# Low halves of the split weights: a subtraction on VectorE or GpSimd replaced by a negated copy on ScalarE and an adding DMA

## The chip, the core and the metric

The kernel runs on one core of one Trainium2 chip. The metric is the device time of one execution in microseconds (us). The median of three timed runs of the kernel before the change is 998.04 us (995.92 to 1000.73). The profile below is of another single execution.

## What is computed

One inference step of a hybrid decoder layer for a prompt of 512 tokens and a sample group of 8 x 8 tokens (576 token columns in all) with the same weights:

```python
hn = rmsnorm(x, norm1_w) * (1 + sc1) + sh1
u = hn @ w_in                                    # split into z, xbc, dt, q, k, v, o, ig, fg, xr, gr
y_ssd = ssd_chunked(causal_conv(xbc), dt, ...)   # Mamba-2 heads, states carried over chunks of 128
y_ml = mlstm_chunked(q, k, v, ig, log_sigmoid(fg), ...)
y_lru = lru_scan(causal_conv(xr), ...) * gelu(gr)
x = x + g1 * (concat(y_ssd, y_ml, y_lru) @ w_out)
hn = rmsnorm(x, norm2_w) * (1 + sc2) + sh2
x = x + g2 * (relu(hn @ mlp_up) ** 2 @ mlp_down)
y = rmsnorm(x, final_norm_w)                     # outputs: y and the new states of the three mixers
```

All inputs are float32. The large products keep float32 accuracy by splitting both operands into a high part, rounded to the reduced format fp32r that TensorE multiplies, and a low part, the exact rest. A product is then three matmuls: high x high, high x low, low x high.

## The kernel before

**Blocks and units.** The weights lie in DRAM as 124 blocks of 128 x 1024 numbers (512 KB): eight 128 x 128 tiles, one for each eighth of the contraction. Block 0 is the gates' weights and isn't split. Blocks 1 to 44 belong to `w_in`, 45 to 60 to `w_out`, 61 to 124 to the MLP. One block is one *unit* on TensorE (PE): for each of the eight tiles six matmuls of 288 columns (`mm_k`, L156 to L166, all at L164): two halves of the tokens with the high weights and the high activations, two with the high weights and the low activations, and two with the low weights (`wl`) and the high activations. So the first matmul that reads `wl` is the fifth of its unit, and the unit's last matmul reads it too.

**How a block is made ready.** `w_load` (L122) queues a DMA of the block from SyncE's queue (SP) into a buffer `raw`, of which there are three. `w_prep` (L132) then makes the two parts: ScalarE (ACT) copies `raw` into `wh` with rounding to fp32r (L150), and a subtraction gives `wl = raw - wh` (L152). The subtraction runs on GpSimd (POOL) for blocks 7 to 32 (`WL_POOL`, L1483) and on VectorE (DVE) for the others; block 3 has its own code (L141 to L146). `wh` and `wl` have three buffers each (`W_BUFS`). When PE starts the unit of block b, the program asks for block b + 2 to be prepared (`PREP = 2`), so `wh` and `wl` of b + 2 take the buffers that block b - 1 has just left.

**Stages.** Up to about 60 us: loads, the first norm and modulation, blocks 1 to 3. To about 470 us: the units of `w_in`, with the mixers between them (convolutions, SSD, mLSTM, RG-LRU), called the mixer stage here. Then 16 units of `w_out`, and from about 568 us the MLP. The last units and the final norm end the program.

**What sets the order.** Each engine runs its own queue strictly in order. The queues' order comes from a scheduler with a timing model that runs when the program is built, apart from the first and the last stretch, where the source fixes it. An instruction that waits holds up everything behind it on its engine. For POOL this covers the DMAs that it issues: the scratch stores `scr_cum` (L524), `scr_nm` (L561) and `scr_ends` (L588) and the outputs at L658, L987, L1146 and L1172. In the mixer stage DVE does most of the elementwise work, the convolution at L626 and L651 above all (taps multiplied and added, 128 x 600), and ACT evacuates the convolution's PSUM banks (L611 to L614).

Of the kernel before, what the change touches and what calls it, by code (L numbers as in the profile page):

```python
# [22 lines left out]
FT = mybir.dt.float32  # L23
FR = mybir.dt.float32r
BF = mybir.dt.bfloat16
AF = mybir.ActivationFunctionType
OP = mybir.AluOpType
# [40 lines left out]
class Kernel:  # L68
# [63 lines left out]
    def w_prep(self, upto):  # L132
        nc = self.nc
        while self.w_next_split <= min(upto, NBLK - 1):
            b = self.w_next_split
            self.w_load(b)
            raw = self.w_raw.pop(b)
            m = raw.shape[2]
            if b == 0:
                self.w_split[b] = raw  # L140
            elif b == 3:  # L141
                hl = [[self.T("wt", FR)[:, :512].rearrange("p (k m) -> p k m", k=4) for _ in range(2)] for _ in range(2)]
                for (hi, lo), src in zip(hl, (raw[:, :4], raw[:, 4:])):
                    nc.scalar.activation(hi, src, AF.Copy)
                    nc.vector.tensor_tensor(lo, src, hi.bitcast(FT), op=OP.subtract)
                self.w_split[b] = (lambda k, t=hl: t[k // 4][0][:, k % 4], lambda k, t=hl: t[k // 4][1][:, k % 4], m)  # L146
            else:
                hi = self.wpool.tile([128, 8, m], FR, name=self.name("wh"), tag="wh", bufs=W_BUFS)
                lo = self.wpool.tile([128, 8, m], FR, name=self.name("wl"), tag="wl", bufs=W_BUFS)
                nc.scalar.activation(hi, raw, AF.Copy)  # L150
                eng = nc.gpsimd if b in WL_POOL else nc.vector
                eng.tensor_tensor(lo, raw, hi.bitcast(FT), op=OP.subtract)  # L152
                self.w_split[b] = (lambda k, t=hi: t[:, k], lambda k, t=lo: t[:, k], m)
            self.w_next_split += 1

# [1324 lines left out]
W_BUFS = 3  # L1480
RAW_BUFS = 3
CONV = "addd"
WL_POOL = range(7, 33)  # L1483
ON_POOL = ('fin', 's0', 'S', 'rmax', 'gu1', 'gu2', 'cf2', 'vm')
TAIL = 2, 1, 2

# [152 lines left out]
```

## Time and profile before

| | |
|---|---|
| median of three runs | 998.04 us |
| profiled execution, device time | 995.4 us |
| its span, first to last instruction | 993.6 us |
| PE busy | 959.5 us, 97% |
| DVE / ACT / POOL busy | 590.2 / 399.8 / 203.8 us |
| moved by DMA | 119.62 MB |

The profiled execution took 995.4 us, of which 1.8 us lie outside the span. The median of the timed runs is 2.6 us above it. A row of a group view gives line, engine, operation, written tile <- read tiles, shape, count, busy time and mean duration, and behind the bar the idle time of the engine just before these instructions with what ended it. PE's matmuls overlap in the pipeline, so two that are shown at 0.43 us start 0.27 us apart.

### The profile page before, as it was taken

What the parts mean: (1) busy time and instruction counts of PE and PEld (TensorE: products, weight loads), DVE (VectorE), ACT (ScalarE), POOL (GpSimd) and SP (SyncE); (2) the same over time, 40 slices, a digit from 0 to 9 for tenths busy, and PEclk for the clock granted to TensorE, in tenths of its full rate; (3) what the DMA queues carried; (4) which work ended last, traced back from release to release, by engine and by line L of the source; (5) the groups of instructions that cost most, each with busy time, mean ns of one, the idle gap of its engine ahead of it and who ended that gap; (6) DMA issues with size and microseconds to landing.
All of it is one profiled execution on the core that took longest, in us unless ns stands there. A gap on an engine that the chain in (4) does not pass through costs nothing.

```text
span 993.6 us, 18146 instructions
## 1 busy us (share of the span) xinstructions
PE 959.5 (97%) x7369; PEld 904.1 (91%) x7370; DVE 590.2 (59%) x1180; ACT 399.8 (40%) x741; POOL 203.8 (21%) x220
## 2 busy tenths in 40 slices
PE   8999789889999999999999999999999999999996
PEld 5889778777788899999999999999999999999996
DVE  4669897887788377468444455533553355335544
ACT  3454744453646674345222234312441144114320
POOL 2836454532355532020000000000000000000032
PEclk8999999998999999999999999999999999999998
DMA  9721254654464333444222322222222222222202
GB/s 343 294 86 64 81 186 133 246 173 137 131 223 153 105 137 129 140 131 162 91 98 105 110 86 84 74 79 84 85 86 85 86 85 76 76 83 85 85 23 96
DMA packets 51220, 119.62 MB, mean 120 GB/s; under 512 B 6956, under 2 KB 17468, under 8 KB 51136
## 3 DMA queue, kind: packets, MB, share of 16 engines
q1 hardware_dynamic: 47024, 111.06, 32.7%
q10 hardware_dynamic: 3744, 6.85, 1.8%
q8 instruction: 58, 0.95, 0.4%
q0 software_dynamic: 368, 0.55, 0.2%
q14 instruction: 26, 0.21, 0.1%
HBM read 108.68 MB, written 9.76 MB: 119 GB/s over the span
## 4 chain that ended last, share of the span: by engine, by line
PE 76%; DVE 10%; ACT 4%; issue 3%; DMA 1%; POOL 0%; POOLq 0%; DVEq 0%; ACTq 0%
PE g L164 66%; DVE r L626 3%; PE adap L218 1%; PE g L1363 1%; DMA nmb<-scr_nm 1%; PE py L729 1%; PE lg L1129 1%; DVE att L707 1%; PE ps L734 1%; PE py L732 1%; DVE nmb L924 1%; DVE xbc L651 0%; DVE sp_e L494 0%; PE adas L228 0%; ACT r L620 0%
## 5 line engine op out<-in xcount | busy, mean ns | idle before, releaser
L150 ACT ACTIVATE wh<-raw 128x1024 fp32r<-128x1024 f32 x123 | 130.1, 1058 | 333.9 <-PE g L164 309.4
L164 PE MATMUL g<-hnh,wh 128*128 128x288 f32 x688 | 153.1, 302 | 10.1 <-ACT r L614 8.0
L164 PE MATMUL g<-hnh,wl 128*128 128x288 f32 x688 | 152.1, 299 | 0.6 <-DVE wl L152 0.6
L164 PE MATMUL g<-hnl,wh 128*128 128x288 f32 x688 | 151.8, 299 | 0.0
L152 DVE TENSOR_TENSOR wl<-raw,wh 128x1024 fp32r<-128x1024 f32 x97 | 118.7, 1225 | 29.5 <-ACT wh L150 29.4
L164 PEld LDWEIGHTS g<-hnh,wh 128*128 128x128 f32 x688 | 110.4, 189 | 19.3 <-ACT r L614 9.2
L164 PEld LDWEIGHTS g<-hnh,wl 128*128 128x128 f32 x688 | 111.6, 189 | 2.7 <-issue 1.2
L164 PEld LDWEIGHTS g<-hnl,wh 128*128 128x128 f32 x688 | 111.7, 189 | 0.8 <-issue 0.4
L164 PE MATMUL g<-h2h,wh 128*128 128x288 f32 (+1 forms) x512 | 110.9, 297 | 0.0
L164 PE MATMUL g<-h2l,wh 128*128 128x288 f32 (+1 forms) x512 | 110.9, 298 | 0.0
L164 PE MATMUL g<-h2h,wl 128*128 128x288 f32 (+1 forms) x512 | 110.0, 296 | 0.0
L307 DVE SCALAR_TENSOR_TENSOR xr<-g,modt,xr 128x288 f32<-128x288 f32 x38 | 19.7, 518 | 141.2 <-PE g L164 141.2
L164 PE MATMUL g<-hh,wl 128*128 128x288 f32 x480 | 102.9, 295 | 0.0
L164 PE MATMUL g<-hh,wh 128*128 128x288 f32 x480 | 102.5, 295 | 0.0
L164 PE MATMUL g<-hl,wh 128*128 128x288 f32 x480 | 102.4, 295 | 0.0
L1405 POOL TENSOR_SCALAR xr<-xr,vec 128x576 f32<-128x576 f32 (+2 forms) x8 | 15.2, 1900 | 383.8 <-ACT sqa L1237 363.4
L152 POOL TENSOR_TENSOR wl<-raw,wh 128x1024 fp32r<-128x1024 f32 x26 | 69.0, 2653 | 80.3 <-ACT wh L150 61.4
L164 PEld LDWEIGHTS g<-h2h,wl 128*128 128x128 f32 x512 | 83.4, 188 | 0.0
L164 PEld LDWEIGHTS g<-h2h,wh 128*128 128x128 f32 x512 | 83.1, 189 | 0.1
L164 PEld LDWEIGHTS g<-h2l,wh 128*128 128x128 f32 x512 | 83.0, 188 | 0.0
L164 PEld LDWEIGHTS g<-hh,wh 128*128 128x128 f32 x480 | 77.0, 188 | 0.0
L164 PEld LDWEIGHTS g<-hh,wl 128*128 128x128 f32 x480 | 77.0, 188 | 0.0
(399 smaller groups left out, 1652.7 us busy)
## 6 DMA issues: line engine op xcount, KB each, us to landing
raw<-w SPq DMA_DIRECT2D x124, 512.0 KB, 3.5
ada<-ada SPq DMA_DIRECT2D x32, 512.0 KB, 5.6
ada<-ada SPq DMA_DIRECT2D x32, 256.0 KB, 5.9
cumb<-scr_cum SPq DMA_DIRECT2D x16, 256.0 KB, 5.6
s<-s SPq DMA_DIRECT2D x16, 256.0 KB, 4.7
ssm_s<-s ACTq DMA_DIRECT2D x16, 256.0 KB, 2.9
x<-x SPq DMA_DIRECT2D x8, 288.0 KB, 4.7
xr<-x SPq DMA_DIRECT2D x8, 288.0 KB, 3.9
```

Source lines behind the costliest of these rows:

```text
L150: nc.scalar.activation(hi, raw, AF.Copy)
L152: eng.tensor_tensor(lo, raw, hi.bitcast(FT), op=OP.subtract)
L164: self.nc.tensor.matmul(pg.h[h][:m, :e], w(k), xx[:, h * HALF:h * HALF + e], start=start and n == 0, stop=stop and n == 2)
L218: nc.tensor.matmul(ps[32 * j:32 * j + 32, :256], self.cs[:, k, :], ks(k), start=k < 4, stop=k >= 4)
L307: self.nc.vector.scalar_tensor_tensor(dst[:, :HALF], pg.h[0][:, :HALF], gate[:, 0:1], x[:, :HALF], op0=OP.mult, op1=OP.add)
L626: nc.vector.scalar_tensor_tensor(a[:, :n], r[:, j:j + n], wcols[:, j:j + 1], a[:, :n], op0=OP.mult, op1=OP.add)
L707: self.eng("att").tensor_scalar(E[:, h * 128:(h + 1) * 128], cums[h2][:, h * 128:(h + 1) * 128], self.col1[:, c, hd:hd + 1], 0.0, op0=OP.a ...
L729: nc.tensor.matmul(o, xdt[:, h * 64:(h + 1) * 64], att[h // 4][:, hs], start=True, stop=not c)
L732: nc.tensor.matmul(o, S[:, h * 64:(h + 1) * 64], ce[h // 4][:, hs], start=False, stop=True)
L734: nc.tensor.matmul(pst, cb[:, 128:256], xend[:, :512], start=True, stop=True)
L924: self.eng("nmb").tensor_scalar(E[:, tk(c)], nmb[:, tk(c)], ecol(c), 0.0, op0=OP.add, op1=OP.min)
L1405: self.eng("fin").tensor_scalar(x, x, self.v("fnw")[:, o:o + 1], None, op0=OP.mult)
```

## The change

For blocks 9 to 124 (except that block 3 is untouched anyway) `wl` isn't subtracted any more. ACT makes a second copy of `raw`, with scale -1 and the same rounding, into `wl`, which then holds the negated high part. POOL then issues a DMA that reads the same block from DRAM a second time and adds it to `wl`, element by element (`accum_op`). The sum is again block minus high part. Blocks 1, 2 and 4 to 8 are subtracted on DVE, so blocks 7 and 8 go from POOL to DVE.

```diff
                 nc.scalar.activation(hi, raw, AF.Copy)
-                eng = nc.gpsimd if b in WL_POOL else nc.vector
-                eng.tensor_tensor(lo, raw, hi.bitcast(FT), op=OP.subtract)
+                if b < WL_DMA:
+                    nc.vector.tensor_tensor(lo, raw, hi.bitcast(FT), op=OP.subtract)
+                else:
+                    nc.scalar.activation(lo, raw, AF.Copy, scale=-1.0)
+                    nc.gpsimd.dma_start(lo, self.io["w"][b - 1].rearrange("p (k m) -> p k m", k=8), accum_op=OP.add)
...
-WL_POOL = range(7, 33)
+
+WL_DMA = 9
```

In the changed kernel L154 is the negated copy and L155 the adding DMA; lines behind them are three higher than before, and from L1484 on four.

POOL's queue early in the mixer stage, around the store `scr_nm`, before:

```order
L152 TENSOR_TENSOR wl_1330<-raw_1130,wh_1329 128x1024
L561 DMA scr_nm<-nm_1110 4x576
L565 DMA m_out<-mo 4x9
L609 MEMSET r_1291 128x3
L610 COPY r_1291<-vec 128x8x3
L635 COPY cso<-r_1291 128x27
L588 DMA scr_ends<-ends 36x12
```

and with the change:

```order
L155 DMA wl_1333<-w 128x1024
L564 DMA scr_nm<-nm_1111 4x576
L612 MEMSET r_1294 128x3
L568 DMA m_out<-mo 4x9
L613 COPY r_1294<-vec 128x8x3
L638 COPY cso<-r_1294 128x27
L591 DMA scr_ends<-ends 36x12
```

The issue of the adding DMA stands where the subtraction stood; the two rows of `m_out` and a memset change places.

DVE's queue at the start of the mixer stage, where blocks 7 and 8 are now subtracted, before:

```order
L651 SCALAR_TENSOR_TENSOR xbc_720<-r_707,r_713 128x512
L653 SCALAR_TENSOR_TENSOR xbc_720<-r_707,r_713 128x64
L651 SCALAR_TENSOR_TENSOR xbc_736<-r_723,r_729 128x512
L653 SCALAR_TENSOR_TENSOR xbc_736<-r_723,r_729 128x64
L626 SCALAR_TENSOR_TENSOR r_745<-r_739,cwh,r_745 128x600 x2
L626 SCALAR_TENSOR_TENSOR r_833<-r_827,cwh,r_833 128x600
L626 SCALAR_TENSOR_TENSOR r_745<-r_739,cwh,r_745 128x600
L626 SCALAR_TENSOR_TENSOR r_833<-r_827,cwh,r_833 128x600 x2
```

and with the change:

```order
L654 SCALAR_TENSOR_TENSOR xbc_720<-r_707,r_713 128x512
L656 SCALAR_TENSOR_TENSOR xbc_720<-r_707,r_713 128x64
L152 TENSOR_TENSOR wl_850<-raw_760,wh_849 128x1024
L654 SCALAR_TENSOR_TENSOR xbc_736<-r_723,r_729 128x512
L656 SCALAR_TENSOR_TENSOR xbc_736<-r_723,r_729 128x64
L629 SCALAR_TENSOR_TENSOR r_745<-r_739,cwh,r_745 128x600 x2
L629 SCALAR_TENSOR_TENSOR r_833<-r_827,cwh,r_833 128x600
L629 SCALAR_TENSOR_TENSOR r_745<-r_739,cwh,r_745 128x600
L629 SCALAR_TENSOR_TENSOR r_833<-r_827,cwh,r_833 128x600
L152 TENSOR_TENSOR wl_930<-raw_762,wh_929 128x1024
L629 SCALAR_TENSOR_TENSOR r_833<-r_827,cwh,r_833 128x600
```

The two subtractions stand between the convolution's operations.

ACT's queue in the MLP, two units of the up-projection and then the first of the down-projection (`r` is the unit's result on its way through the squared ReLU, `hh` its high part), before:

```order
L150 ACTIVATE wh_8178<-raw_8042 128x1024
L1261 ACTIVATE r_8163<-r_8163,shw_8164 128x512
L1262 ACTIVATE r_8163<-r_8163 128x64
L1264 ACTIVATE hh_8170<-r_8163 128x576
L150 ACTIVATE wh_8245<-raw_8109 128x1024
L1261 ACTIVATE r_8230<-r_8230,shw_8231 128x512
L1262 ACTIVATE r_8230<-r_8230 128x64
L1264 ACTIVATE hh_8237<-r_8230 128x576
L150 ACTIVATE wh_8305<-raw_8176 128x1024
```

and with the change:

```order
L150 ACTIVATE wh_8257<-raw_8119 128x1024
L154 ACTIVATE wl_8258<-raw_8119 128x1024
L1264 ACTIVATE r_8242<-r_8242,shw_8243 128x512
L1265 ACTIVATE r_8242<-r_8242 128x64
L1267 ACTIVATE hh_8249<-r_8242 128x576
L150 ACTIVATE wh_8325<-raw_8187 128x1024
L154 ACTIVATE wl_8326<-raw_8187 128x1024
L1264 ACTIVATE r_8310<-r_8310,shw_8311 128x512
L1265 ACTIVATE r_8310<-r_8310 128x64
L1267 ACTIVATE hh_8317<-r_8310 128x576
L150 ACTIVATE wh_8386<-raw_8255 128x1024
L154 ACTIVATE wl_8387<-raw_8255 128x1024
```

The negated copy stands right behind the rounded one, ahead of the unit's own evacuation. In the mixer stage other ACT work often lies between the two.

## The prediction

> **What bounds the kernel now.** I read the busy totals first, then the stretches of the span one by one, then in each stretch what PE and the engines before it wait for.
>
> The page's head, and the busy time by stretch (each cell: busy us and instructions; the last three columns are granted TensorE clock, mean busy share of the DMA engines, GB/s):
>
> ```profile
> PE 959.5 (97%) x7369; PEld 904.1 (91%) x7370; DVE 590.2 (59%) x1180; ACT 399.8 (40%) x741; POOL 203.8 (21%) x220
> ...
> core 0: us, PE busy (x) PEld busy (x) DVE busy (x) ACT busy (x) POOL busy (x), PEclk, DMA share, GB/s
> 60.00:150.00 90.00, 80.49 (x619) 75.81 (x620) 83.18 (x142) 52.14 (x106) 44.89 (x54) 0.98 0.32 100
> 150.00:270.00 120.00, 111.50 (x931) 94.42 (x933) 92.08 (x232) 58.08 (x144) 47.93 (x37) 0.97 0.50 161
> 270.00:380.00 110.00, 107.25 (x808) 95.88 (x801) 79.27 (x174) 68.92 (x154) 49.49 (x44) 1.00 0.43 153
> 380.00:470.00 90.00, 90.00 (x735) 83.96 (x735) 58.08 (x110) 45.35 (x93) 12.28 (x16) 1.00 0.45 147
> 470.00:568.00 98.00, 98.00 (x740) 98.00 (x740) 41.30 (x77) 24.79 (x29) 3.30 (x10) 1.00 0.29 104
> 568.00:930.00 362.00, 362.00 (x2710) 361.71 (x2709) 173.84 (x317) 112.75 (x154) 1.17 (x1) 1.00 0.23 82
> ```
>
> From 380 to 930 us PE has no gap: nothing that is taken off another engine there can shorten the program. The gaps lie in the mixer stage: 90 - 80.5 = 9.5 us up to 150 us, 8.5 us up to 270 us, 2.75 us up to 380 us, 20.8 us in all. That is the most this change can gain. Up to 150 us DVE is the fullest engine behind PE, 83.2 of 90 us.
>
> What the low parts cost now (duration in ns as least, median, most; the second pair of rows is the same line seen from the engines that wait for it):
>
> ```profile
> L152 DVE TENSOR_TENSOR wl<-raw,wh x97: 1204/1224/1578, 23.0 to 962.9; 128x1024 fp32r<-128x1024 f32 x97
> ...
> L152 POOL TENSOR_TENSOR wl<-raw,wh x26: 2328/2394/5690, 68.0 to 345.6; 128x1024 fp32r<-128x1024 f32 x26
> ...
>   PEld g L164: 0.8, 1
> ...
>   PE g L164: 0.6, 1
> ```
>
> PE waited for a low part 1.4 us in the whole program. So the subtraction itself is not on PE's path; it matters only by what it takes from DVE. What POOL's share takes from DVE shows where the two overlap, here in the timeline, POOL first:
>
> ```profile
> 107.14 2.58 POOL L152 TENSOR_TENSOR wl<-raw,wh 128x1024 fp32r<-128x1024 f32 x1 [3.27 <-ACT wh L150]
> ```
>
> ```profile
> 107.55 2.81 DVE L626 SCALAR_TENSOR_TENSOR r<-r,cwh,r 128x600 f32<-128x600 f32 x1
> ...
> 111.17 0.69 DVE L651 SCALAR_TENSOR_TENSOR xbc<-r,r 128x512 f32<-128x512 f32 x1
> ...
> 111.91 0.84 DVE L626 SCALAR_TENSOR_TENSOR r<-r,cwh,r 128x600 f32<-128x600 f32 x1
> ```
>
> The same operation takes 0.84 us alone and 2.81 us beside the subtraction: DVE lost nearly the whole time that POOL was at work. The groups of 60 to 150 us, on DVE and on ACT, show how much that is and who stands behind it:
>
> ```profile
> L626 DVE SCALAR_TENSOR_TENSOR r<-r,cwh,r 128x600 f32<-128x600 f32 x33 | 34.5, 1057 | 3.5 <-ACT r L620 3.2
> L651 DVE SCALAR_TENSOR_TENSOR xbc<-r,r 128x512 f32<-128x512 f32 x11 | 9.2, 840 | 3.6 <-ACT r L649 3.5
> L707 DVE TENSOR_SCALAR att<-cumb,col 128x128 f32<-128x128 f32 x24 | 7.5, 383 | 0.0
> ```
>
> ```profile
> L150 ACT ACTIVATE wh<-raw 128x1024 fp32r<-128x1024 f32 x10 | 10.5, 1050 | 1.9 <-PE g L164 1.9
> ...
> L649 ACT ACTIVATE r<-r 128x600 f32<-128x600 f32 x11 | 7.7, 702 | 15.3 <-DVE r L626 15.2
> ```
>
> ```profile
> PEld g L164 <- ACT r L614: 9.2, 4, 4.5
> PE g L164 <- ACT r L614: 8.0, 4, 4.3
> ```
>
> ACT stands 15.2 us behind DVE's L626, and PE 8.0 us behind ACT's evacuation L614 (the last row; the row above it is the same gaps, seen by the weight loads). ACT works in order, so a late DVE holds the evacuation, and that holds PE.
>
> **The change part by part.** *POOL's subtractions go.* 26 of them leave POOL. DVE's stretch goes with them. In 60 to 150 us: L626 33 x (1.057 - 0.84) = 7.2 us. L651 11 x (0.840 - 0.69) = 1.65 us. For L707 the undisturbed value comes from 150 to 270 us, 0.278 us, so 24 x (0.383 - 0.278) = 2.5 us:
>
> ```profile
> L707 DVE TENSOR_SCALAR att<-cumb,col 128x128 f32<-128x128 f32 x40 | 8.2, 278 | 0.0
> ...
> L924 DVE TENSOR_SCALAR nmb<-nmb,col 128x128 f32<-128x128 f32 x8 | 3.9, 542 | 0.8 <-DMA nmb<-scr_nm 0.8
> ```
>
> Together 11.3 us. Between 150 and 270 us the clear case is L924, of L707's shape: 8 x (0.542 - 0.278) = 2.1 us.
>
> *Blocks 7 and 8 go to DVE*, 2 x 1.22 = 2.4 us, both between the convolution's operations. Net relief of DVE up to 150 us: 8.9 us.
>
> *DVE's 90 other subtractions go* (97 less the 7 left): 90 x 1.22 = 110 us, all behind 350 us, where PE has no gap worth naming. Worth nothing.
>
> *ACT's negated copy comes*, 116 times. The trace has no such copy; the nearest row is its twin L150, 1.05 us, same shape and types, so +122 us. From 380 us on PE is full and ACT under 51% busy (45.35 of 90 us is the most): hidden, and if that cover were gone it would cost 1.05 us per unit. In 60 to 150 us there are 10 copies, 10.5 us, while ACT idles 15.2 us behind L626 alone. They hurt where DVE waits for ACT: 3.2 us at L620. The bounds are nothing and one copy ahead of each of the 11 convolution inputs, 11.6 us. Nearer is the low end, since a wait exists already only for 3.2 us; I take two copies, 2.1 us.
>
> *POOL's DMA issue comes.* Nearest rows: POOL's own DMAs, and the loads, with KB each and median us from issue to landing:
>
> ```profile
> L987 POOL DMA_DIRECT2D mc_p<-C x4: 581/606/629, 201.2 to 423.6; - x4
> ...
> raw<-w SPq DMA_DIRECT2D x124, 512.0 KB, 3.5
> ...
> c<-c SPq DMA_DIRECT2D x8, 260.0 KB, 7.9
> ```
>
> 0.61 us per issue instead of 2.39 us. It waits for the negated copy, 1.05 us later than the subtraction did, so POOL is free again 0.7 us sooner. Behind it in POOL's queue stand the store `scr_nm` and the mixers' products, which DVE and the mLSTM loads wait for; they lose nothing.
>
> *The adding DMA's latency* is not in the trace. At the least it lands like `raw`, 3.5 us. At the most, like the slowest load, 7.9 us for 260 KB, so 15.6 us for 512 KB. I take 3.5 plus a second pass over the engines for reading the destination plus a `raw` load in front. One pass is the DMA share 0.23 of a unit. The unit is the distance of these three rows of ACT's timeline:
>
> ```profile
> 654.34 1.06 ACT L150 ACTIVATE wh<-raw 128x1024 fp32r<-128x1024 f32 x1 [5.29 <-PE g L164]
> 660.68 1.06 ACT L150 ACTIVATE wh<-raw 128x1024 fp32r<-128x1024 f32 x1 [5.29 <-PE g L164]
> 667.03 1.06 ACT L150 ACTIVATE wh<-raw 128x1024 fp32r<-128x1024 f32 x1 [5.29 <-PE g L164]
> ```
>
> ```profile
> 654.40 0.42 PE L164 MATMUL g<-hh,wh 128*128 128x288 f32 x2
> 654.67 0.42 PE L164 MATMUL g<-hl,wh 128*128 128x288 f32 x2
> 654.93 0.43 PE L164 MATMUL g<-hh,wl 128*128 128x288 f32 x2
> ```
>
> A unit takes 6.35 us, so a pass takes 0.23 x 6.35 = 1.5 us, and the landing 3.5 + 1.5 + 1.5 = 6.5 us.
>
> Its cover: the `wh` that starts at 654.34 is for the block whose unit starts two units on, right behind 667.03. The low part is first read 0.6 us into a unit (654.34 to 654.93), so at 667.6. From the end of `wh`, 655.40, that is 12.2 us. Less the copy (1.06) and the issue (0.61) this leaves **10.5 us** for the landing. 6.5 us is hidden. Before this the margin was larger, but PE waits for nothing in both cases.
>
> *The engines' load.* 116 x 512 KB are read once more. Per unit of 6.35 us the `raw` load takes 1.5 us, so up to 4.9 us are free for the adding DMA. At the least it takes one pass, 1.5 us; at the most the 15.6 us above. I take two passes, 2.9 us. In 150 to 270 us, where the share is 0.50, eight POOL subtractions make way for about as many adding DMAs, 8 x 2.9 / 120 = 0.20 more. That leaves room, but loads of the mixers that collide take longer; I charge 1 us.
>
> [...] No run here has shown an adding DMA yet.
>
> **The sum.** Up to 150 us: 8.9 - 2.1 = 6.8 us less on the way DVE, ACT, PE; PE has 9.5 us of gaps there, of which 8.0 us hang on L614. I count two thirds, 4.5 us, since other waits then end last. Behind 150 us: -2.1 us for L924, +1 us for colliding loads. From 380 us: 0. In all -5.6 us: 995.4 - 5.6 = 989.8 us against the profiled execution's own time; the median of the runs is 2.6 us higher, so 992.4, rounded **993 us**. The forecast's own range is 987 to 997.
>
> **Rivals.**
> *Hidden anyway, 998 us.* DVE's relief ends at another wait: the queues' order changes with the change, and 20.8 us of gaps are spread over the stretch. For it: only 8.0 us of PE's wait has a name. Against it: the stretched operations lie on the way to just that wait.
>
> *The adding DMA lands late, 1060 us.* Place: each unit from 470 us on. The three buffers tie a block's copy to the unit three before: `wh` 1.06, copy 1.06, issue 0.61, landing L, then 5.75 us from the first read of the low part to the unit's end make up three units. So a unit takes (8.5 + L) / 3, and this decides from L = 10.5 us on. There are 498 / 6.35 = 78 units to 968 us, so each further us costs 26 us. At 13 us, the middle between 10.5 and 15.6, that is 2.5 x 26 = +65 us. The same happens if an adding DMA takes over 4.9 us of the engines. For it: no row shows such a DMA, and the upper bound of 15.6 lies beyond. Against it: `raw` of the same size lands in 3.5 us, three times faster than needed.
>
> *The mixers' loads pay, 1006 us.* The chain of waits holds a load of `nmb`:
>
> ```profile
> 174.09 8.67 DMA nmb<-scr_nm
> ```
>
> If the adding traffic doubles this landing and ACT's copies cost five waits of 1.06 us instead of two, the sum is -5.6 + 8.7 + 3.2 = +6.3 us, and with a second such load a little more: about 1006. It decides where a load is started too late for its reader. Against it: the share of 0.50 leaves half of the engines free.
>
> *More than forecast, 984 us.* 14 of the 20.8 us of gaps go, since 26 POOL operations less also relieve DVE behind 150 us in places that the rows' means don't show.
>
> **How the numbers follow.** Forecast 0.48, hidden 0.20, late 0.17, loads 0.10, more 0.05. A measurement of this kernel tells about 0.5%, 5 us, from no change, so faster means under 993 us, which is the middle of my forecast. Faster: 0.30 of the forecast's 0.48, with 0.05 and 0.01 of the hidden case, 0.36. Same: 0.18 + 0.18 + 0.02 of the loads' = 0.38. Slower: 0.17 + 0.08 + 0.01 = 0.26. The range goes from 985, the edge of the best case, to 1035, which takes in the loads' case and the late case up to L of about 12 us; some 0.15 stays outside.
>
> **What would show it.** Right: L626 in 60 to 150 us falls from 1057 to about 850 ns; PE's wait for L614 falls from 8.0 to some 3 us; ACT is busy about 520 us, DVE about 450 us; the adding DMAs land in 5 to 8 us and PE waits for no `wl`; three `wh` rows of the MLP stay 6.35 us apart. Wrong: PE idle in front of the fifth matmul of a unit with the adding DMA as releaser, `wh` rows further apart (late DMA); `nmb` or `cumb` landing much later than before with DVE waiting for it (loads); L626 at 850 ns with the gaps of PE unchanged (hidden); an issue on POOL well above 0.6 us, with POOL's products behind it.

## The result and the profile after

The change made the kernel slower: 1006.57 us (median of 4 runs, 1005.17 to 1011.1) against 996.98 us before (4 runs), a ratio of 1.0105, 95% interval 1.0072 to 1.0139, which is 10.5 us (7.2 to 13.9). The ratio is estimated from the single runs and isn't the quotient of the two medians. The prediction was 993 us in a range of 985 to 1035, with faster and same as the two likelier signs: the time lies in the range, but on the other side of the kernel before. The profiled execution took 1006.16 us, with a span of 1004.4 us.

The page's line of busy times and the same stretches as in the prediction, after the change (busy us and instructions of each engine; then granted clock, DMA share, GB/s):

```profile
PE 969.2 (96%) x7370; PEld 910.3 (91%) x7370; DVE 451.6 (45%) x1090; ACT 499.5 (50%) x857; POOL 225.6 (22%) x310
```

```profile
60.00:150.00 90.00, 83.95 (x646) 78.00 (x648) 70.48 (x148) 59.76 (x114) 21.84 (x52) 0.96 0.62 162
150.00:270.00 120.00, 111.72 (x913) 92.81 (x909) 79.06 (x237) 68.67 (x156) 35.67 (x39) 0.96 0.69 192
270.00:380.00 110.00, 103.42 (x735) 93.05 (x736) 58.39 (x144) 70.37 (x149) 34.31 (x45) 0.93 0.66 177
380.00:470.00 90.00, 88.73 (x712) 82.37 (x711) 45.84 (x108) 53.90 (x106) 19.66 (x23) 1.00 0.79 206
470.00:568.00 98.00, 98.00 (x747) 96.80 (x746) 27.22 (x67) 41.75 (x51) 14.72 (x29) 1.00 0.82 190
568.00:930.00 362.00, 362.00 (x2707) 361.73 (x2707) 110.39 (x258) 157.78 (x207) 49.62 (x57) 1.00 0.73 165
```

DVE lost 139 us of work, as the change says. ACT gained 100, less than the 121 us that the copies' own rows add up to, since neighbouring operations on ACT overlap: in the MLP a negated copy starts 0.97 us after a rounded copy that takes 1.06. Up to 150 us PE is better off (83.95 us busy instead of 80.49). From 270 to 380 us it is worse: 6.6 us of gaps instead of 2.75, a granted clock of 0.93 instead of 1.00, and 735 matmuls instead of 808. From 470 us on PE is full, as before. So all that was lost was lost in the mixer stage.

Two kinds of loss can be told apart in these rows. PE's gaps up to 470 us are hardly longer than before: 6.05 + 8.28 + 6.58 + 1.27 = 22.2 us against 20.8. The granted clock lost much more. The missing share of the clock times the stretch is 90 x 0.04 + 120 x 0.04 + 110 x 0.07 = 16.1 us after and 90 x 0.02 + 120 x 0.03 = 5.4 us before. These 10.7 us (good to some 2 us, as the clock has two digits) are about the whole loss.

The groups of 60 to 150 us after the change, for the lines that the relief was counted on, and one row of the waits of the same stretch:

```profile
L629 DVE SCALAR_TENSOR_TENSOR r<-r,cwh,r 128x600 f32<-128x600 f32 x33 | 27.1, 837 | 7.2 <-ACT r L623 6.9
...
L654 DVE SCALAR_TENSOR_TENSOR xbc<-r,r 128x512 f32<-128x512 f32 x11 | 7.5, 682 | 2.7 <-ACT r L652 2.7
...
L710 DVE TENSOR_SCALAR att<-cumb,col 128x128 f32<-128x128 f32 x24 | 5.1, 283 | 3.1 <-DMA cumb<-scr_cum 3.1
```

```profile
PE g L167 <- ACT r L617: 2.1, 1, 2.1
```

The relief is there as priced: 837 ns instead of 1057 for the convolution, 283 instead of 383 for `att`, and PE waits 2.1 us for the convolution's evacuation instead of 8.0. The prices stand in the same rows: DVE waits 6.9 us for ACT's L623 where it waited 3.2, and 3.1 us for the load of `cumb` where it didn't wait at all.

What the adding DMAs did, in rows of the page (first on POOL: busy, mean ns; then KB and median us from issue to landing):

```profile
L155 POOL DMA_DIRECT2D wl<-w x116 | 101.4, 874 | 553.5 <-ACT wl L154 504.2
...
raw<-w SPq DMA_DIRECT2D x124, 512.0 KB, 4.2
wl<-w POOLq DMA_DIRECT2D x116, 512.0 KB, 8.0
...
cumb<-scr_cum SPq DMA_DIRECT2D x16, 256.0 KB, 7.8
s<-s SPq DMA_DIRECT2D x16, 256.0 KB, 6.0
```

and the last two of before:

```profile
cumb<-scr_cum SPq DMA_DIRECT2D x16, 256.0 KB, 5.6
s<-s SPq DMA_DIRECT2D x16, 256.0 KB, 4.7
```

The adding DMA lands in 8.0 us in the median (5.4 to 10.6), below the 10.5 us of cover but for the slowest. The mixers' loads `cumb` and `s` land 2.2 and 1.3 us later than before.

To see where the time went, I took the end of each unit's last matmul in both profiles, counted from the end of block 6's unit. At block 11 the change is 11.4 us ahead. It loses 5.3 us at block 14, is 12.8 us ahead again at block 21, loses 7.1 and 5.8 us at blocks 22 and 23, and 9.0 us at block 29. From block 35 on it stays some 10 us behind. The largest single loss, on PE after the change (start, duration; in brackets the idle time before and its releaser):

```profile
337.05 2.10 PE L1132 MATMUL lg<-xc,lw 128*128 128x288 f32 x8
340.38 1.07 PE L221 MATMUL adap<-ada,cs 128*32 128x256 f32 x16 [1.23 <-ACT r L1135]
343.11 1.02 PE L231 MATMUL adas<-vec,adarow 128*128 128x9 f32 x4 [1.66 <-ACT adarow L223]
343.98 0.83 PE L167 MATMUL g<-hnh,wh 128*128 128x288 f32 x2
344.61 0.68 PE L167 MATMUL g<-hnl,wh 128*128 128x288 f32 x2
345.09 0.68 PE L167 MATMUL g<-hnh,wl 128*128 128x288 f32 x2
...
349.72 0.42 PE L167 MATMUL g<-hnh,wh 128*128 128x288 f32 x2
349.98 0.42 PE L167 MATMUL g<-hnl,wh 128*128 128x288 f32 x2
```

and the same work before:

```profile
336.15 1.07 PE L218 MATMUL adap<-ada,cs 128*32 128x256 f32 x16
337.15 0.40 PE L164 MATMUL g<-hnl,wh 128*128 128x288 f32 x1
...
340.05 0.42 PE L164 MATMUL g<-hnh,wh 128*128 128x288 f32 x2
340.31 0.51 PE L228 MATMUL adas<-vec,adarow 128*128 128x9 f32 x4
340.67 0.51 PE L164 MATMUL g<-hnl,wh 128*128 128x288 f32 x2
```

`adas` needs a row that ACT copies out of `adap` (L223). Before, 23 matmuls of a unit lie between the two, so that copy costs nothing. After the change `lg`, `adap` and `adas` stand back to back, PE waits 1.23 and 1.66 us, and then the next unit's pairs of matmuls start 0.48 us apart instead of 0.27 until 349.4 us. The granted clock of that stretch, after and then of the same unit before (first column the stretch, last but two the clock):

```profile
343.80:352.90 9.10, 9.10 (x50) 9.08 (x50) 3.50 (x6) 1.93 (x5) 1.96 (x1) 0.69 0.61 163
```

```profile
337.70:344.70 7.00, 7.00 (x57) 6.84 (x60) 3.90 (x6) 2.91 (x5) 2.96 (x2) 1.00 0.67 226
```

Both programs issue the same matmuls; the scheduler put them in another order. Three theories follow for the 10 us: the **order** of the queues, ACT's **copies**, or the **loads** that share the transfer engines with the adding DMAs.

### The profile page after: what moved, and what is told of

The parts are those of the page before. It is cut to its first block, busy times and chain, and to the rows that moved or that the text cites. A ratio compares the mean times of both kernels' runs of the same rounds, so it can differ in the third digit from the quotient of the medians.

```text
span 1004.4 us, 18380 instructions
## 1 busy us (share of the span) xinstructions
PE 969.2 (96%) x7370; PEld 910.3 (91%) x7370; DVE 451.6 (45%) x1090; ACT 499.5 (50%) x857; POOL 225.6 (22%) x310
## 3 DMA queue, kind: packets, MB, share of 16 engines
q0 software_dynamic: 17072, 61.38, 34.0%
## 4 chain that ended last, share of the span: by engine, by line
PE 67%; ACT 3%; DVE 1%; issue 1%; POOL 0%; POOLq 0%; ACTq 0%; DVEq 0%
PE g L167 62%; PE g L1366 1%; PE adap L221 1%; PE lg L1132 0%; ACT wh L150 0%; PE adas L231 0%; ACT wl L154 0%; ACT L1154 0%; DVE r L1170 0%; ACT la L1138 0%; ACT r L1154 0%; DVE fo L1459 0%; PE ms L1422 0%; PE ms L273 0%; ACT ii L1135 0%
## 5 line engine op out<-in xcount | busy, mean ns | idle before, releaser
L155 POOL DMA_DIRECT2D wl<-w x116 | 101.4, 874 | 553.5 <-ACT wl L154 504.2
L167 PE MATMUL g<-hnh,wh 128*128 128x288 f32 x688 | 156.5, 307 | 6.8 <-ACT r L617 3.6
L167 PEld LDWEIGHTS g<-hnh,wh 128*128 128x128 f32 x688 | 112.6, 192 | 16.0 <-issue 6.4
L154 ACT ACTIVATE wl<-raw 128x1024 fp32r<-128x1024 f32 x116 | 121.2, 1045 | 0.1
L167 PEld LDWEIGHTS g<-hl,wh 128*128 128x128 f32 x480 | 76.9, 188 | 0.0
```

The costliest lines, as they stand in the source:

```text
L154: nc.scalar.activation(lo, raw, AF.Copy, scale=-1.0)
L155: nc.gpsimd.dma_start(lo, self.io["w"][b - 1].rearrange("p (k m) -> p k m", k=8), accum_op=OP.add)
L167: self.nc.tensor.matmul(pg.h[h][:m, :e], w(k), xx[:, h * HALF:h * HALF + e], start=start and n == 0, stop=stop and n == 2)
```

## The experiments

Times below are against runs of the kernel before on the same chip; a ratio r is also given as (r - 1) x 997 us. Such a difference is uncertain by 2 to 3.5 us to either side, and the step from one program to another by 3.5 to 5 us. To keep a queue's order, the programs marked "held" chain the instructions of an engine in the order of a table, with edges that order but don't wait:

```diff
         down_last()
+        self.set_order()
...
+    def set_order(self):
+        by = {}
+        for i in list(self.tc.nc.cur_bb.bb.instructions)[self.n_before:]:
+            if type(i).__name__ != "BassTilePoolBoundary":
+                by.setdefault(str(i.engine).split(".")[-1], []).append(i)
+        table = json.loads(zlib.decompress(base64.b85decode(ENGINE_ORDER)))
+        for e, places in table.items():
+            for p, q in zip(places, places[1:]):
+                self.tc.add_manual_dep(by[e][q], by[e][p].name, mybir.DependencyInfo(
+                    mybir.DependencyClass.NoSync, mybir.DependencyReason.DATA), reason="order")
```

### The whole change, in the order of before

The change's diff, with PE, DVE, ACT and SP held in the order of before.

> The whole change, but PE, DVE, ACT and SP keep the order of their queues from the kernel before; the negated copy stands right behind the rounded copy on ACT, and the adding DMAs are placed on POOL by the scheduler. Order theory (the +9.6 us come from the queues that the scheduler made for the changed program, where for instance the gates' matmuls of the rows before block 29 stand back to back): the relief of DVE, 11.4 us up to block 11 in the trace after, stays for the most part, and the kernel is 3 to 9 us faster than before. Copies theory (116 negated copies of 1.05 us on ACT push its evacuations back): 4 to 10 us slower than before, as the change. Loads theory (adding DMAs delay cumb, nmb and s): 3 to 10 us slower, with DVE waiting for cumb and nmb.

Measured: 993.51 us, ratio 0.9969 (0.9947 to 0.9991), 3.1 us faster. In this order the change pays a little. 13.6 us of the change's result are the order of the queues. Copies and loads theory both expected slower. But little or nothing is left of a gain that stood at 8 to 10 us up to block 17 in this run's profile: 3.1 us by the timed runs, 1.3 us by the profile at the end of block 44. The gain went at block 18 and block 24, and the waits of 150 to 270 us and of 270 to 380 us show by whom:

```profile
PEld pc L829 <- DMA s<-s: 4.4, 2, 3.2
...
PE pc L829 <- DMA s<-s: 2.3, 1, 2.3
```

```profile
PE pv L944 <- DVE s L842: 2.9, 1, 2.9
```

PE waits for the load of `s`, for which it didn't wait before, and later for DVE's update of the same state. Around both waits the clock is lower: 0.93 from 179 to 204 us and 0.77 from 280 to 295 us, where pairs of matmuls start 0.48 us apart from 287.94 to 288.90 us.

### The copies alone

```diff
                 nc.scalar.activation(hi, raw, AF.Copy)
+                if b >= NEG_FROM:
+                    nc.scalar.activation(lo, raw, AF.Copy, scale=-1.0)
                 eng = nc.gpsimd if b in WL_POOL else nc.vector
```

All queues held in the order of before, `NEG_FROM = 9`.

> The kernel before with its own subtractions, plus the 116 negated copies on ACT (written into wl and then overwritten by the subtraction, so they are pure load), all queues in the order of before. Order theory: 0 to 3 us slower than before. Copies theory: 8 to 12 us slower. Loads theory: 0 to 2 us slower.

Measured: 1005.34 us, ratio 1.0086 (1.0056 to 1.0116), 8.6 us slower. The copies do cost, four times the 2.1 us of the prediction, as the copies theory had it. Here each subtraction also waits for the copy, so I measured them a second way below.

### The order alone

`WL_POOL = range(9, 33)`, all queues held in the order of the changed kernel.

> No negated copy and no adding DMA: subtractions as before (7 and 8 on DVE, 9 to 32 on POOL where the change has the adding DMA, 33 to 124 on DVE), but all queues in the order of the changed kernel. Order theory: 8 to 16 us slower than before (POOL's subtractions stretch DVE as before, and the order costs what it cost in the change). Copies theory and loads theory: within 3 us of before.

Measured: 1019.66 us, ratio 1.0217 (1.0184 to 1.025), 21.6 us slower. The order of the changed kernel costs even more without the change, and more than the 8 to 16 us that the order theory expected. In this run's profile the losses lie at the same units as in the changed kernel: 6.5 us at block 14, 5.2 and 4.3 at 22 and 23 (behind a gain of 5.9 at 21), 6.7 at 29, and another 5.7 at 34, where the changed kernel lost little.

### The change for the late blocks alone

`WL_DMA = 33`, POOL and DVE subtract as before for the others, order of before held on PE, DVE, ACT and SP.

> The change only for blocks 33 to 124 (1 to 32 are subtracted as before), queues of PE, DVE, ACT and SP in the order of before. The prediction's step 'nothing from 380 us on' and the order theory: within 2 us of before, MLP units stay 6.35 to 6.4 us apart. Copies theory: 0 to 2 us slower, since ACT is under 51 per cent busy there. Loads theory: 1 to 4 us slower, since the last loads of the mixers lie between 350 and 470 us.

Measured: 997.04 us, ratio 1.0005 (0.9976 to 1.0033). From block 33 on the change is hidden, with all its DMAs, to within some 3 us. The run also shows that holding the queues costs nothing visible by itself.

### The terms one by one, in the order of before

Four programs with PE, DVE, ACT and SP held in the order of before take the change apart. The first keeps the copy and leaves out the adding DMA:

```diff
-                eng = nc.gpsimd if b in WL_POOL else nc.vector
-                eng.tensor_tensor(lo, raw, hi.bitcast(FT), op=OP.subtract)
+                if b < WL_DMA:
+                    nc.vector.tensor_tensor(lo, raw, hi.bitcast(FT), op=OP.subtract)
+                else:
+                    nc.scalar.activation(lo, raw, AF.Copy, scale=-2.0 ** -13)
```

> In the order of before, the subtractions of blocks 9 to 124 replaced by ACT's second copy alone, with scale -2^-13, and no adding DMA: wl holds a scaled high part instead of the low part. Against the kernel with the whole change in the same order (3.1 us faster than before) this takes away the DMA traffic and the POOL issues and keeps the copies. Loads theory (what that kernel lost again at the units of blocks 18 and 24, 4.8 and 5.8 us in its profile, comes from the loads of s that land late): 6 to 11 us faster than before. Copies theory (the copies took it back): 0 to 4 us faster.

Measured: 984.92 us, ratio 0.9881 (0.9852 to 0.991), 11.9 us faster, nearest to the loads theory's 6 to 11.

The second has a plain second load in place of copy and adding DMA:

```diff
+                else:
+                    nc.gpsimd.dma_start(lo, self.io["w"][b - 1].rearrange("p (k m) -> p k m", k=8).bitcast(FR))
```

> In the order of before, the subtractions of blocks 9 to 124 replaced by a plain second load of the block into wl from POOL's queue, without a copy on ACT and without adding: wl holds the whole block instead of the low part. Against the whole change in this order it takes away the copies and the read of the destination. Loads theory: at least the part of a plain pass stays, 2 to 6 us faster than before. Copies theory: 6 to 11 us faster.

Measured: 978.95 us, ratio 0.9833 (0.9799 to 0.9867), 16.6 us faster, more than either theory expected.

The third makes no low part:

```diff
-                lo = self.wpool.tile([128, 8, m], FR, name=self.name("wl"), tag="wl", bufs=W_BUFS)
+                lo = self.last_low if b >= WL_DMA else self.wpool.tile([128, 8, m], FR, name=self.name("wl"), tag="wl", bufs=W_BUFS)
```

> In the order of before, no low part is made for blocks 9 to 124: their matmuls read the low part of block 8. No copy, no adding DMA, no subtraction: the ceiling of what the removal of the subtractions can give in this order. All theories: 7 to 12 us faster than before, since 8 us were gained up to block 17 in the kernel with the whole change in this order; if it is less than 5, other waits end last and the relief itself was overrated.

Measured: 975.69 us, ratio 0.9794 (0.9767 to 0.9821), 20.5 us faster, twice what was expected. The stretches of its profile:

```profile
60.00:150.00 90.00, 87.79 (x712) 81.82 (x704) 75.23 (x161) 54.89 (x111) 17.67 (x45) 1.00 0.44 135
150.00:270.00 120.00, 116.56 (x970) 98.66 (x968) 85.28 (x251) 66.58 (x164) 28.62 (x33) 0.99 0.54 173
270.00:380.00 110.00, 109.44 (x827) 100.09 (x824) 68.75 (x151) 67.62 (x144) 28.20 (x38) 1.00 0.42 144
```

Of the 20.8 us of PE's gaps 6.2 are left, and the granted clock rises from 0.98, 0.97 and 1.00 to 1.00, 0.99 and 1.00. So the subtractions were worth far more than the two thirds of DVE's stretch up to 150 us, and half of the gaps that went (7.3 of 14.6 us) lay behind 150 us, where the prediction had found 2.1 us.

The fourth has the adding DMA without the copy, into three fixed tiles:

```diff
+                else:
+                    nc.gpsimd.dma_start(lo, self.io["w"][b - 1].rearrange("p (k m) -> p k m", k=8), accum_op=OP.add)
...
-                lo = self.wpool.tile([128, 8, m], FR, name=self.name("wl"), tag="wl", bufs=W_BUFS)
+                lo = self.low_tiles[b % 3] if b >= WL_DMA else self.wpool.tile([128, 8, m], FR, name=self.name("wl"), tag="wl", bufs=W_BUFS)
```

> In the order of before, blocks 9 to 124 get no subtraction and no copy, but an adding DMA into one of three fixed tiles: wl holds a running sum of blocks instead of the low part. So far, in this order, no low part at all gave 20.5 us, ACT's copies alone cost 8.6 of it, a plain second load 3.9, copies and adding DMAs together 17.4. Loads theory (the adding DMA costs by its own time on the transfer engines): 10 to 14 us faster than before, some 9 us short of the ceiling. Chain theory (it costs because copy, issue and landing stand in a row behind each other, and only with the copy): 15 to 18 us faster, as the plain load.

Measured: 986.8 us, ratio 0.9885 (0.9853 to 0.9916), 11.5 us faster: 9.0 us short of the ceiling, as the loads theory had it. The cost is there without the copy, so it isn't the chain of copy, issue and landing. Who pays it can be read from the waits from 60 to 480 us: DVE waits 8.4 us for the load of `nmb` where it waits 3.1 in the third program, and 3.2 us for `cumb` where it doesn't wait there. The landings of the plain load and of the adding DMA, each in its own program without copies:

```profile
L157 POOL DMA_DIRECT2D wl<-w x116 | 63.4, 547 | 593.8 <-PE g L169 579.8
...
raw<-w SPq DMA_DIRECT2D x124, 512.0 KB, 4.6
wl<-w POOLq DMA_DIRECT2D x116, 512.0 KB, 3.9
...
cumb<-scr_cum SPq DMA_DIRECT2D x16, 256.0 KB, 6.7
```

```profile
L158 POOL DMA_DIRECT2D wl<-w x116 | 101.4, 874 | 568.8 <-PE g L170 554.4
...
raw<-w SPq DMA_DIRECT2D x124, 512.0 KB, 6.7
wl<-w POOLq DMA_DIRECT2D x116, 512.0 KB, 7.1
...
cumb<-scr_cum SPq DMA_DIRECT2D x16, 256.0 KB, 8.3
```

Adding makes the landing 7.1 us instead of 3.9 and the issue 0.874 us instead of 0.547, and the loads beside it later: `raw` 6.7 instead of 4.6, `cumb` 8.3 instead of 6.7. The plain second load cost 20.5 - 16.6 = 3.9 us against the third program, so adding costs some 5 us more than loading.

Together, against the kernel before and in its order:

| term | from | us |
|---|---|---|
| subtractions gone | third program | -20.5 |
| ACT's copies | first less third: -11.9 + 20.5 | +8.6 |
| adding DMAs | fourth less third: -11.5 + 20.5 | +9.0 |
| sum | | -2.9 |
| whole change in this order | first experiment | -3.1 |
| order of the changed kernel | change less first experiment: 10.5 + 3.1 | +13.6 |
| the change | | +10.5 |

The terms add up, and the copies cost 8.6 us by both ways of measuring. As each term is uncertain by 3 to 5 us, agreement to 0.2 us is partly luck. The line of the order is a difference, so that the last line must come out; measured by itself, with the subtractions in place, the changed kernel's order cost 21.6 us.

### The copy on DVE

```diff
-                    nc.scalar.activation(lo, raw, AF.Copy, scale=-1.0)
+                    nc.vector.tensor_scalar(lo, hi.bitcast(FT), -1.0, None, op0=OP.mult)
```

Order of before held.

> The whole change in the order of before, but the negated copy is made on DVE (high part times -1) instead of ACT, at the place where DVE or POOL subtracted. DVE keeps an operation per block of 0.6 to 1.2 us instead of 1.22, ACT gets none. Copies theory: 4 to 9 us faster than before. Loads theory: 1 to 4 us faster, as the whole change in this order. If DVE's added 24 operations in the mixer stage matter: no gain.

Measured: 998.24 us, ratio 1.0003 (0.998 to 1.0026): no gain. DVE's copy takes 0.69 us, and the program is 3.4 us slower than with ACT's copies, though the intervals just overlap. The expectation that fitted was its last one, that DVE's operations in the mixer stage matter. Against the adding DMA without any copy (11.5 us faster) the copy is dear on both engines.

### The early blocks alone

`WL_DMA = range(9, 18)`, `WL_POOL = range(18, 33)`, order of before held.

> Copy and adding DMA for blocks 9 to 17 alone, POOL subtracts 18 to 32 and DVE 33 to 124 as before (7 and 8 on DVE), queues in the order of before. In the whole change in this order the gain stood at 8 to 10 us at the unit of block 17 and shrank at blocks 18 and 24. If those later losses come from the copies and adding DMAs of blocks behind 17: 6 to 10 us faster than before. If they are late bills of the early gain (something else ends last there anyway): 0 to 4 us faster.

Measured: 987.6 us, ratio 0.9909 (0.9873 to 0.9945), 9.1 us faster, and faster than both kernels. The gain up to block 17 stays when no copy and no adding DMA comes behind it. So what the whole change lost at blocks 18 and 24 in this order comes from the later copies and DMAs.

### Another threshold

`WL_DMA = 7` instead of 9, all queues by the scheduler.

> The changed kernel with one number changed: copy and adding DMA from block 7 on instead of 9, queues as the scheduler makes them for that program. By the terms of the prediction's sum this is worth 2.4 us at most (two subtractions less on DVE against two copies and two DMAs). Order theory: since PE's queue then differs from the change's in some 360 rows, it may land anywhere within 12 us on either side of it: more than 4 us away from the change is expected. Loads and copies theory: within 3 us of the change.

Measured: 1004.13 us, ratio 1.0061 (1.0035 to 1.0086), 4.4 us faster than the change itself. That is just beyond the 4 us of the order theory, but the step is uncertain by about as much, so it proves little alone.

### Only PE's queue in the order of before

The change, PE held in the order of before; the scheduler makes the other queues around it.

> The whole change with only PE's queue held in the order of before; the scheduler makes the other queues around it. If PE's own order (the gates' matmuls back to back ahead of block 29, the mixers' matmuls ahead of blocks 14, 22 and 23) carries the loss: 0 to 5 us faster than before, as with all queues held (3.1 us faster). If ACT's and DVE's orders carry it: 4 to 12 us slower than before.

Measured: 988.56 us, ratio 0.9913 (0.9888 to 0.9939), 8.7 us faster. Holding PE's order, with the other queues made around it, turns 10.5 us slower into 8.7 us faster, 19.2 us. That the other queues may follow the change gives 5.6 us more than with all of them held. The stretches up to 380 us:

```profile
60.00:150.00 90.00, 86.13 (x682) 79.94 (x676) 72.79 (x153) 61.55 (x117) 23.64 (x52) 0.98 0.64 162
150.00:270.00 120.00, 114.88 (x960) 95.61 (x956) 83.94 (x246) 71.78 (x165) 38.74 (x42) 1.00 0.74 207
270.00:380.00 110.00, 104.68 (x772) 94.45 (x764) 63.50 (x155) 75.54 (x157) 36.46 (x46) 0.98 0.74 196
```

Against the changed kernel PE's gaps fall from 20.9 to 14.3 us, and the lost clock from 16.1 to 90 x 0.02 + 110 x 0.02 = 4.0 us. So PE's order costs by waits and, as much or more, by the clock.

The ends of the units against before, in us (minus is earlier), from the profiles, counted from the end of block 6's unit:

| block | change | order alone | change, order held | change, PE's order held |
|---|---|---|---|---|
| 11 | -11.4 | -5.1 | -8.1 | -7.0 |
| 14 | -3.9 | +3.5 | -8.2 | -10.1 |
| 21 | -12.8 | +0.2 | -7.9 | -13.6 |
| 23 | +0.1 | +9.7 | -6.9 | -14.7 |
| 24 | +2.1 | +10.5 | -1.0 | -12.4 |
| 28 | -0.8 | +8.4 | -0.8 | -12.3 |
| 29 | +8.2 | +15.1 | -0.7 | -12.3 |
| 34 | +9.7 | +20.9 | -1.2 | -8.7 |
| 44 | +9.9 | +21.1 | -1.3 | -8.7 |

### Which rows of PE's queue

Four programs have the changed kernel's PE rows at one place and all else as in the one before, its other queues held too.

> The kernel with the whole change and only PE's queue from before (8.7 us faster than before), with all its queues held; alone the PE rows around the unit of block 29 (1837 to 2003 of the queue) stand as in the changed kernel: the gate matmuls, the modulation's two products and block 29's matmuls without matmuls of a unit between them. Order theory, place by place: the changed kernel lost 9.0 us at this unit in its profile, so this loses 5 to 10 us against the PE order of before (4 us faster to 1 us slower than the kernel before). If PE's order matters only as a whole, or through the other queues: within 3 us of the PE order of before, 6 to 11 us faster than the kernel before.

Measured: 991.93 us, ratio 0.9965 (0.994 to 0.9991), 5.2 us slower than with PE's order of before. Its timeline at the place:

```profile
323.57 1.07 PE L225 MATMUL adap<-ada,cs 128*32 128x256 f32 x16
326.46 0.81 PE L235 MATMUL adas<-vec,adarow 128*128 128x9 f32 x4 [1.82 <-ACT adarow L227]
327.12 0.83 PE L171 MATMUL g<-hnh,wh 128*128 128x288 f32 x2
327.75 0.68 PE L171 MATMUL g<-hnl,wh 128*128 128x288 f32 x2
...
330.15 0.44 PE L171 MATMUL g<-hnh,wh 128*128 128x288 f32 x2
330.43 0.44 PE L171 MATMUL g<-hnl,wh 128*128 128x288 f32 x2
```

A wait of the same kind, and slow matmuls behind it as in the changed kernel (pairs 0.48 us apart from 327.75 to 330.15 us). But the profile doesn't keep the loss. Against PE's order of before, these rows gain 3.1 us up to block 28 before they lose 6.5 at block 29, and at block 34 they lose 2.0 us where the order of before loses 3.6. At the end of block 44 both stand alike, 9.1 and 8.7 us ahead of the kernel before. Up to block 24, where the two programs are the same, their profiles differ by up to 2.2 us. So the timed runs give 5.2 us, uncertain by 3.6, and the profile gives nothing.

> As the one for block 29, with PE's rows 602 to 747, from the unit of block 12 to that of block 14, as in the changed kernel: the SSD products stand nearly back to back, where before a unit's matmuls lie between them. Order theory, place by place: the changed kernel lost 2.8 and 5.3 us there in its profile, so 5 to 9 us slower than with the PE order of before (4 us faster to 1 us slower than the kernel before). Otherwise within 3 us of it, 6 to 11 us faster than the kernel before.

Measured: 987.67 us, ratio 0.9923 (0.9896 to 0.9949), 1.0 us slower than with PE's order of before, inside the uncertainty. Alone these rows do nothing.

> As the two others, with PE's rows 1386 to 1499, at the units of blocks 22 and 23, as in the changed kernel. Its profile lost 7.1 and 5.8 us there, but 5.8 us of that only gave back what it had gained at block 21. Order theory, place by place: 3 to 8 us slower than with the PE order of before (6 us faster to 1 us slower than the kernel before). Otherwise within 3 us of it.

Measured: 984.87 us, ratio 0.989 (0.9864 to 0.9916), 2.3 us faster than with PE's order of before and 11.0 us faster than before. Nothing is lost there either: in its profile the 5.2 us lost at block 22 follow a gain of 5.8 us at block 21. This is the lowest time of the programs that compute everything, though its interval overlaps those of the early blocks alone and of PE's order alone.

> The whole change with PE's queue from before and the other queues held as in that kernel (8.7 us faster than before), but PE's rows 602 to 1576, from the unit of block 12 to that of block 24, as in the changed kernel. Alone, the rows of blocks 12 to 14 cost 1 us and those of 22 and 23 nothing. If the loss of the changed kernel up to block 24 (13.5 us from its best point, the end of block 11, to the end of block 24 in its profile) is a sum of many places in PE's rows there: 6 to 13 us slower than with the PE order of before (3 us faster to 4 us slower than the kernel before). If PE's rows need the other queues of the changed kernel to cost something: within 3 us of it, 6 to 11 us faster than the kernel before.

Measured: 994.6 us, ratio 0.9959 (0.9935 to 0.9983), 4.6 us slower than with PE's order of before. Together the rows of blocks 12 to 24 cost 4.6 us, between the two expectations; in the profile it is 6.7 us at the end of block 44. The two places tried alone make up none of it (1.0 us slower and 2.3 us faster).

The counterpart of the first of these puts the good rows at block 29 into the changed kernel, with PE's queue held so and the others by the scheduler:

> The changed kernel with PE's rows 1837 to 2003, around the unit of block 29, put back to the order of before; all the rest of PE's queue as in the changed kernel, the other queues by the scheduler (they come out as in the changed kernel but for some 10 rows). The counterpart of the run that put the changed rows into the good order and lost 5.2 us. Order theory, place by place: 4 to 9 us faster than the changed kernel, 1 to 6 us slower than the kernel before. Otherwise as the changed kernel, 8 to 12 us slower than before.

Measured: 1002.22 us, ratio 1.0062 (1.0032 to 1.0092), 4.3 us faster than the change (2.7 us in the profile at the end of block 44). By the timed runs this one place is worth 4 to 5 us, taken out or put in; by the profiles 0 to 3.

So of the 19.2 us of PE's order, some 5 lie at block 29 by the timed runs (0 to 3 by the profiles) and 5 to 7 in blocks 12 to 24, each good to about 3.5 us. The rest appears only with the changed kernel's other queues or with rows elsewhere. How the cost is shared out over PE's rows stays open.

### Both remedies

The early blocks alone, with only PE's queue held.

> Copy and adding DMA for blocks 9 to 17 alone (9.1 us faster than before with all queues held), with only PE's queue held in the order of before and the others made by the scheduler. If the scheduler's other queues suit the change, as the step from all queues held to PE's alone did for the whole change (3.1 to 8.7 us faster): 9 to 15 us faster than before. If that step was special to the many adding DMAs: 6 to 10 us faster.

Measured: 987.52 us, ratio 0.9908 (0.9874 to 0.9942), 9.2 us faster. The two remedies don't add up. With few adding DMAs the scheduler's other queues differ less from before: in the traces some 12 rows on DVE and 18 on ACT, against 79 and 55 with the whole change.

## Why the prediction was wrong

**The step that failed** is the sum's: it carries DVE's relief over to the end of the program as if PE's queue stayed as it was, and prices the new order at nothing ("From 380 us: 0. In all -5.6 us"). The order costs 13.6 us and sets the sign, by waits of PE and by the lower clock: in the stretches to 470 us the gaps grew by 1.4 us, relief included, and the lost clock by 10.7. The prediction had no term for the clock. It had quoted how rows of POOL, DVE and ACT move, but not PE's. Its rival "hidden anyway" named the queues' order, as something that uses up the gain and at 998 us. In the same queue order the change measured 3.1 us faster, and with only PE's order held 8.7.

Step by step:

- **The bound.** "That is the most this change can gain", 20.8 us: the ceiling measured 20.5. The two agree less well than they look, since 6.2 us of the gaps stayed and the rest came with the higher granted clock.
- **DVE's relief** was right in its rows (L626 about 850 ns: 837; the wait for L614 some 3 us: 2.1) and mis-sized in the sum: 4.5 us up to 150 us and 2.1 behind it, where the removal is worth 20.5. The prediction itself had named this under "more than forecast", at 0.05.
- **ACT's copies**, 2.1 us taken of bounds 0 to 11.6: 8.6 measured. "A wait exists already only for 3.2 us" looked at one wait, L620. ACT is also waited for by the mixers: with the copies alone, from 225 to 310 us, DVE waits 6.3 us for ACT's `C` instead of 3.4, and PE 1.4 us for `num`, for which it didn't wait before.
- **Loads that collide**, 1 us: 9.0 measured. The prediction reasoned from the half of the engines that stays free. A load with a reader waiting is late all the same: `cumb` lands after 7.8 us instead of 5.6, `s` after 6.0 instead of 4.7.
- **The adding DMA**: landing 8.0 us for 6.5, inside 3.5 to 15.6 and below the margin of 10.5. PE waits for no `wl` from a DMA there (in the order of before it does once, for 1.7 us). Its share of the engines in the MLP is (0.73 - 0.23) x 6.35 = 3.2 us per unit for 2.9. So the rival "lands late", 1060 us, was wrong, and the test with the late blocks alone shows the MLP hidden, as predicted.
- **The issue on POOL**, 0.61 us: 0.874. A plain load's issue took 0.547 in the same place, so the row taken was right for a plain DMA. No run separates its price from the 9.0 us of the adding DMAs.
- **The rival "the mixers' loads pay"**, 1006 us at 0.10, hit the time by a sum of other terms: it had five waits for copies and a late `nmb`, +6.3 us in all. Copies and adding DMAs cost 17.6 us, the larger relief pays that back, and the order makes the loss. That it came near was luck for the most part. Its named place was in part right: from 60 to 480 us DVE waits 8.5 us for `nmb` instead of 2.9.
- **Slips of the working**, none of which moves the forecast by 1 us: PE waited for a low part 0.6 us and not 1.4, since the 0.8 us of the weight loads are the same gap; 92 subtractions of blocks 33 to 124 leave DVE and not 90, as blocks 7 and 8 were counted apart; 992.4 rounds to 992.

The prediction took two passes of the engines for an adding DMA, the second for reading the destination. That was an estimate: no run shows the reading, only what adding costs in time. From 568 to 930 us the change adds 0.73 - 0.23 = 0.50 to the DMA share. The plain second load, with the same 61.38 MB on POOL's queue, adds half of that:

```profile
568.00:930.00 362.00, 362.00 (x2710) 361.98 (x2709) 113.48 (x264) 111.45 (x155) 31.87 (x58) 1.00 0.50 164
```

0.50 less the 0.23 of before is 0.27, so 1.7 us per unit against the 3.2 us of the adding DMA, and in the two programs without copies the landings stand at 3.9 to 7.1 us.

## What to carry to other kernels

When a scheduler makes the queues, a change of engines is two changes: its terms, and a new order of the bound engine. Compare that engine's queue before and after, look for places where dependent matmuls lost the independent ones between them, and time the change with that queue held before judging it. Read the granted clock of each stretch beside the gaps: here the gaps were 22.2 us against 20.8, the lost clock 16.1 us against 5.4. Idle time on an engine and idle share of the DMA engines are no proof of cover (here ACT's copies cost 8.6 us and the adding DMAs 9.0): price a new operation by who waits for that engine in the stage. And apply such a change only where it pays: nine of the 116 blocks gave 9.1 us, where all of them gave 3.1 in the same order.

## What the runs showed that was not expected

- **PE ran slower for several us behind short waits.** Behind idle times of 1.23 and 1.66 us (with small matmuls between them) pairs of matmuls started 0.48 us apart instead of 0.27 from 344.6 to 349.4 us, at a granted clock of 0.50 (0.99 from 349.4 to 352.9 us); behind a single one of 1.82 us for about 3 us. At block 29 twelve pairs took 5.74 us (343.98 to 349.72) where 12 x 0.27 is 3.2, so 2.5 us came on top of the waits. That the waits brought the lower clock is read from their order in time; no run tests it by itself.
- **An adding DMA of 512 KB cost 1.6 to 1.9 times a plain one**: landing 7.1 to 3.9 us, engine time 3.2 to 1.7 us, and 0.874 to 0.547 us on POOL to issue it.
- **The removal of the subtractions was worth 20.5 us**, though PE waited for a low part only 0.6 us in the whole program.
